# A decoder trunk on one core: the condition turned into columns on PE, the other vectors carried in the scale weights' rows

## The chip, the cores and the metric

The kernel runs on one core of one Trainium2 chip, in one launch. The metric is the device time of an execution in microseconds (us). A profile is one execution taken by the hardware profiler; in it PE is TensorE (PEld its weight loads), DVE is VectorE, ACT is ScalarE, POOL is GpSimd and SP is SyncE, which here only issues loads. Lines such as L354 are lines of the kernel before the change, unless the text says otherwise.

## The reference

One decoder layer on 512 tokens of width 1024, in float32. A condition vector `c` sets a shift, a scale and a gate for each of two sublayers. What the change touches is the first step of the first sublayer:

```python
cs = jax.nn.silu(c)
mod = cs @ w_ada[l] + b_ada[l]
shift1, scale1, gate1, shift2, scale2, gate2 = [m[:, None, :] for m in jnp.split(mod, 6, axis=-1)]
h = _rmsnorm(x, norm1_g[l]) * (1.0 + scale1) + shift1
proj = h @ w_in[l]
qa, ka, va, qd, kd, vd, ga, gd = jnp.split(proj, points, axis=-1)
```

`proj` then feeds two causal attention branches, one with a sliding window of 128 and learned sinks (8 heads, 2 key heads), one the difference of two softmax maps (4 heads). Each is projected to width 1024, they are merged by sigmoid gates `ga` and `gd`, projected once more and added to `x` times `gate1`. The second sublayer is an RMSNorm with `scale2` and `shift2`, and a gated MLP of width 2816 with a causal convolution of width 3 ahead of the GELU, added times `gate2`. A last RMSNorm ends it.

## The kernel before

Every large product is made of three: each float32 operand is split into a high part (rounded by a cast on ACT) and a low part (what is left, by a subtraction on DVE), and PE adds high·high, high·low and low·high.

The start of the kernel is written by hand, in the order in which each engine is to run it (`manual_schedule`). The features are cut into eight steps of 128 (k = 0 to 7). In this order:

- Loads. One load on ACT's queue brings `columns`, 128 rows of 161 numbers: `c` as 8 columns, the other vectors (biases, norm weights, convolution weights) as the rest, into the tile `cols`. SP's queue brings in turn the four pieces of the transposed `x` (`xT`), the shift weights of step 0 (`adaw0`, j = 1), its scale weights (`w_ada_0`, j = 0), the first 128 rows of the input projection (`w0`), and then the same three for each further step. Each of these is 512 KB.
- The condition. `cs` = silu of the 8 columns, made by an exponential on ACT and three steps on DVE (L255 to L258). PE repeats it along rows into two banks (L262), and DVE copies these to SBUF as `csb`. Ahead of that PE multiplies constants (`keep_warm`, L236).
- The norm of x. ACT squares the pieces of `xT` (L315), DVE adds the two halves of each (L316), and PE sums over features (`sums`, L304). A root on ACT and some small steps on DVE give one number per token, `rst`, which PE turns into a row (L340) in the bank `acc[7]`.
- Scale and shift of step 0. The scale comes from PE (`head_mod`, L296): eight products of `w_ada_0` with `cs`, five ahead of the turning of `rst` and three behind it, into `acc[3]`. The shift comes from DVE as two dot products with `csb` (`shift_half`, L325). Two DVE steps make of them the multiplier (L382) and the addend (L383) of `h`.
- `h` of step 0. DVE multiplies `xT` by the row of `rst` in two halves of 256 tokens (`scale_x`, L348), ACT applies multiplier and addend in two pieces (`h_tile`, L354; result `hThA`, the high part), then once more in full precision (`hf`), and copies the row of `rst` to SBUF (`rstb`, L388). DVE takes `hf` minus the high part (`h_low`).
- Products. 24 products a step into eight banks, `acc[0]` to `acc[7]` (in the trace aka, aqa, av, ava): eight with both high parts, eight with the weights' low part, eight with the low part of `h` (`mm_k`, L365 and L368). In step 0 the first three and the last of each eight take 128 tokens of `h` each (tokens 0 to 127, 128 to 255, 256 to 383 and 384 to 511); the other four take all 512.

For each further step ACT casts the weights (`split_hi`), makes multiplier and addend (`mod_end`, L279 and L280) from dot products on DVE (`mod_rows`), and `h`. What follows (attention, gates, the MLP) is ordered by a scheduler by priorities, with PE's stream again written out; the first two tiles of attention weights (`wqa`, cast at L120) are the first of it.

The lines at which the condition enters:

```python
nc.scalar.dma_start(cols[:, :NCOL], columns)
ccol, bsh, bsc1 = cols[:, 0:8], cols[:, 8:16], cols[:, 16:24]
keep_warm(10)
nc.scalar.activation(cs, ccol, AF.Exp, scale=-1.0)
```

Of the kernel before, what the change touches and what calls it, by code (L numbers as in the profile page):

```python
# [36 lines left out]
VA_AT = 5  # L37
SWA_FILL = (2, 1, 6, 2, 2, 2, 2, 5, 0)
DIFF_FILL = (3, 2, 4, 2)
NCOL = 161  # L40
# [7 lines left out]
def kernel(  # L48
# [4 lines left out]
    columns: bass.AP,  # L53
# [85 lines left out]

    cols = cpool.tile([P, NCOL + 32], F32, name="cols")  # L140
    nc.scalar.dma_start(cols[:, :NCOL], columns)
    ccol, bsh, bsc1 = cols[:, 0:8], cols[:, 8:16], cols[:, 16:24]
    blate, n1g, n2g = cols[:, 24:56], cols[:, 56:64], cols[:, 64:72]
    cv, sublnc = cols[:, 72:160], cols[:, 160:161]
# [108 lines left out]
    keep_warm(10)  # L253
# [40 lines left out]
    def head_mod(a0, a1):  # L294
        for a in range(a0, a1):
            nc.tensor.matmul(  # L296
                acc[3][:, :NB], adaw[0][:, 0, a * P : (a + 1) * P], cs[:, a : a + 1].to_broadcast([P, NB]),
                start=a == 0, stop=a == KT - 1,
            )
# [11 lines left out]
    for p in range(KT // 2):  # L311
        for hf in range(2) if p == 3 else (None,):
            sl = ALL if hf is None else HALVES[hf]
            sq, xx = (a.rearrange("p (a s) -> p a s", a=2)[:, :, sl] for a in (sqs[p], xT[:, p]))
            nc.scalar.activation(sq, xx, AF.Square)  # L315
# [13 lines left out]
    shift_half(0)  # L329
    r0 = pp.tile([P, NT], F32, tag="rs_c", bufs=3, name="r0")  # L330
# [7 lines left out]
    head_mod(0, 5)  # L338
    for t in range(NT):
        nc.tensor.transpose(acc[7][:, t * P : (t + 1) * P], rst[:, t : t + 1].to_broadcast([P, P]), ident)  # L340
    head_mod(5, KT)
# [37 lines left out]
    keep_warm(3)  # L379
    scale_x(0, HALVES[0])  # L380
    m = mods[0]
    nc.vector.tensor_scalar(m[:, 0:1], acc[3][:, 0:1], n1g[:, 0:1], cb[:, 0:1], ALU.mult, ALU.add)  # L382
    nc.vector.scalar_tensor_tensor(m[:, 1:2], m[:, 4:5], m[:, 5:6], bsh[:, 0:1], ALU.add, ALU.add)  # L383
    scale_x(0, HALVES[1])
    for sl in HALVES:
        h_tile(0, 0, sl)
# [1451 lines left out]
    "x", "x_t", "columns", "w_ada_0", "w_ada_t", "w_first", "w_tiles", "swa_sinks", "diff_lambda",  # L1838
# [40 lines left out]
```

## Time and profile before

| | |
|---|---|
| median of 3 runs | 677.56 us (676.93 to 678.12) |
| the profiled execution | 677.26 us, its span 675.4 us |
| PE busy | 665.2 us (98% of the span), 4021 instructions |
| DVE busy | 564.6 us (84%) |
| ACT busy | 400.2 us (59%) |
| POOL busy | 86.4 us (13%) |
| granted TensorE clock, mean | 0.996 |
| moved by DMA | 121.78 MB, mean 180 GB/s |

The span runs from the first to the last instruction; 1.86 us of the profiled execution lie outside it. A matmul's end is modelled, so a busy PE is not PE at its peak; but where PE is busy in every slice, the time is that of its instruction stream. In the chain of waits, read from the last instruction back, PE holds 88% of the span.

### The profile page before, as it was taken

Reading aid. Unit: us, or ns where it says so; the run is one execution under the profiler, and the core shown is the slowest. Engines: PE = TensorE matmul, PEld = TensorE weight load, DVE = VectorE, ACT = ScalarE, POOL = GpSimd, SP = SyncE. Lnnn points to the kernel's source line nnn. Section 1 sums busy time; section 2 is a strip of 40 time slices with the busy share of each in tenths; the row PEclk is TensorE's granted clock in tenths of the full one; section 3 lists DMA queues with packets and bytes.
Section 4 is the critical chain, followed back from the end, with each engine's and each line's share of the span. In section 5 each row is a group of like instructions: output and inputs, shape, how many; then the busy total and the mean of one; then the engine's idle time right before and its main releaser. Section 6 shows DMA issues by size and latency. Waiting matters only on the chain.

```text
span 675.4 us, 10796 instructions
## 1 busy us (share of the span) xinstructions
PE 665.2 (98%) x4021; PEld 591.2 (88%) x4021; DVE 564.6 (84%) x1006; ACT 400.2 (59%) x703; POOL 86.4 (13%) x111
## 2 busy tenths in 40 slices
PE   8999999999999999999999999999999999999995
PEld 7888888888888888888899999999999998888884
DVE  6997996778767688954899998888888899979996
ACT  6678787466645333233696655556655666665664
POOL 2000000002213200010010211011111004441200
PEclk9999999999999999999999999999999999999998
DMA  8962231355266798569275987897786559996803
GB/s 351 408 242 71 87 103 63 127 155 173 93 172 195 233 317 263 196 168 309 68 122 139 226 201 198 204 214 163 186 197 175 128 187 210 197 200 188 158 0 125
DMA packets 72068, 121.78 MB, mean 180 GB/s; under 512 B 4240, under 2 KB 48432, under 8 KB 72016
## 3 DMA queue, kind: packets, MB, share of 16 engines
q1 hardware_dynamic: 53104, 95.04, 41.6%
q0 software_dynamic: 18624, 25.84, 23.0%
q8 instruction: 31, 0.51, 0.3%
q10 hardware_dynamic: 288, 0.21, 0.1%
q14 instruction: 21, 0.17, 0.1%
HBM read 118.97 MB, written 2.11 MB: 179 GB/s over the span
## 4 chain that ended last, share of the span: by engine, by line
PE 88%; issue 7%; DVE 2%; POOL 1%; DMA 1%; ACT 0%; POOLq 0%
PE up L1202 33%; PE dc L1808 7%; PE av L368 3%; PE pga L123 2%; PE pga L125 2%; PE pga L124 2%; PE pgd L125 2%; PE oc L1258 2%; PE pgd L124 2%; PE oc L1259 2%; PE oc L1262 2%; PE pgd L123 2%; PE aqa L365 2%; PE sd L679 2%; PE sw L581 1%
## 5 line engine op out<-in xcount | busy, mean ns | idle before, releaser
L1202 PE MATMUL up<-t,m_whi 128*128 128x256 f32 x512 | 93.1, 283 | 0.0
L1202 PEld LDWEIGHTS up<-t,m_whi 128*128 128x128 f32 x512 | 79.9, 192 | 0.0
L1202 PE MATMUL up<-t,m_wlo 128*128 128x256 f32 x256 | 72.4, 283 | 0.0
L1202 PE MATMUL up<-bh,p_whi 128*128 128x256 f32 x232 | 65.7, 283 | 0.0
L1202 PE MATMUL up<-bl,p_whi 128*128 128x256 f32 x232 | 65.7, 283 | 0.0
L1202 PE MATMUL up<-bh,p_wlo 128*128 128x256 f32 x232 | 65.7, 283 | 0.0
L1202 PEld LDWEIGHTS up<-t,m_wlo 128*128 128x128 f32 x256 | 49.2, 192 | 0.0
L1104 POOL DMA_DIRECT2D s<-in_w_up_dram x21 | 27.0, 1368 | 157.6 <-DMA s<-in_w_up_dram 127.8
L1202 PEld LDWEIGHTS up<-bh,p_whi 128*128 128x128 f32 x232 | 44.5, 192 | 0.0
L1202 PEld LDWEIGHTS up<-bl,p_whi 128*128 128x128 f32 x232 | 44.5, 192 | 0.0
L1202 PEld LDWEIGHTS up<-bh,p_wlo 128*128 128x128 f32 x232 | 44.5, 192 | 0.0
L1132 ACT CAST m_whi<-s 128x1024 fp32r<-128x1024 f32 x31 | 32.5, 1047 | 15.7 <-DVE s L1126 9.1
L795 DVE CUSTOM_DVE_ANT_0 ra<-ra,csb 128x1024 f32<-128x1024 f32 x32 | 38.6, 1219 | 3.0 <-DMA ra<-in_w_ada_t_dram 3.0
L1136 DVE TENSOR_TENSOR m_wlo<-s,m_whi 128x1024 fp32r<-128x1024 f32 x31 | 37.8, 1218 | 1.3 <-ACT m_whi L1132 1.3
L1202 PE MATMUL up<-t,p_whi 128*128 128x256 f32 x176 | 32.2, 283 | 0.0
L1202 PEld LDWEIGHTS up<-t,p_whi 128*128 128x128 f32 x176 | 27.4, 192 | 0.1
L705 ACT ACTIVATE sd<-sd,dmx 128x128 f32<-128x128 f32 (+3 forms) x32 | 17.7, 555 | 14.9 <-DVE dmx L690 14.7
L1132 ACT CAST p_whi<-wa 128x1024 fp32r<-128x1024 f32 x18 | 18.8, 1043 | 12.6 <-DMA s<-in_w_up_dram 7.2
L1209 ACT ACTIVATE gT<-a,cols 128x512 f32<-128x512 f32 x22 | 17.6, 813 | 13.4 <-DVE a L1244 13.0
L1136 DVE TENSOR_TENSOR p_wlo<-wa,p_whi 128x1024 fp32r<-128x1024 f32 x18 | 22.0, 1222 | 4.0 <-ACT p_whi L1132 3.2
L1202 PE MATMUL up<-t,p_wlo 128*128 128x256 f32 x88 | 24.9, 283 | 0.0
L1126 DVE TENSOR_TENSOR s<-s,wa 128x1024 f32<-128x1024 f32 x20 | 24.4, 1218 | 0.1
(551 smaller groups left out, 2037.6 us busy)
## 6 DMA issues: line engine op xcount, KB each, us to landing
ra<-in_w_ada_t_dram SPq DMA_DIRECT2D x32, 512.0 KB, 4.7
wa<-in_w_up_dram SPq DMA_DIRECT2D x22, 512.0 KB, 4.3
s<-in_w_up_dram SPq DMA_DIRECT2D x21, 512.0 KB, 4.7
s<-in_w_up_dram POOLq DMA_DIRECT2D x21, 512.0 KB, 6.6
adaw<-in_w_ada_t_dram SPq DMA_DIRECT2D x15, 512.0 KB, 10.2
a<-in_w_up_dram SPq DMA_DIRECT2D x11, 512.0 KB, 4.9
b<-in_w_down_dram SPq DMA_DIRECT2D x10, 512.0 KB, 3.9
w<-in_w_first_dram SPq DMA_DIRECT2D x8, 512.0 KB, 10.2
```

Source lines behind the costliest of these rows:

```text
L123: nc.tensor.matmul(o, lh, rh, start=start, stop=False)
L124: nc.tensor.matmul(o, lh, rl, start=False, stop=False)
L125: nc.tensor.matmul(o, ll, rh, start=False, stop=stop)
L368: nc.tensor.matmul(acc[i], ht[:, t : t + P], wts[k][w][:, S:], start=start, stop=stop)
L705: nc.scalar.activation(pm[m], pm[m], AF.Exp, bias=mx[:, m : m + 1], scale=-1.0, accum_out=(l0, l1)[m])
L795: nc.vector.tensor_tensor_reduce(r, r, csb, 1.0, 0.0, ALU.mult, ALU.add, late_mod[:, idx : idx + 1])
L1104: nc.gpsimd.dma_start(dst, upblock(*blk), accum_op=ALU.add)
L1126: nc.vector.tensor_add(src, src, R[J, "a11" if name == "m6" else "a12"])
L1132: nc.scalar.copy(W[J, name][0], R[J, SRC[name]])
L1136: nc.vector.tensor_sub(lo, R[J, SRC[name]], hi.bitcast(F32))
L1202: nc.tensor.matmul(o[u], w[:, k, cu], b[:, k], start=name in ("p1", "m5", "p2") and k == 0 and x == 0, stop=k == 3 and x == 2, skip_group_ ...
L1808: nc.tensor.matmul((bank2[u] if o is None else o)[:, sl], a[:, q, cu], b[:, q, sl], start=first_mm and x == 0, stop=last_mm and x == 2, sk ...
```

## The change

`c` is no longer part of `columns`. It is loaded as it lies in memory, 8 rows of 128 numbers (`crow`, 4 KB, on ACT's queue), and PE transposes these rows into 8 columns of a bank that is free then (`acc[2]`), between six and three of the products of constants, which were ten in a row. ACT and DVE read the condition from the bank.

The other vectors, now 153 columns, stand behind the 1024 scale weights in the rows of `w_ada_0`; both come in one load into a tile of their own (`scale0`, 1177 numbers a row) by SP's queue, in the scale weights' place. GpSimd copies the 153 columns to `cols`, and does the scalings of some of them and the product `cb`, which DVE did before. `cols` keeps its size, and the tiles behind `scale0` begin at multiples of 64 bytes as before.

Around it the order changes: the squares of the first piece of `xT` are made in two halves; the second copy of `csb` goes ahead of the last square additions; the addend of `h` is computed ahead of the scaling of `xT`; `h` of step 0 is made in pieces of 128, 128 and 256 tokens.

```diff
-NCOL = 161
+NCOL = 153
...
-    cols = cpool.tile([P, NCOL + 32], F32, name="cols")
-    nc.scalar.dma_start(cols[:, :NCOL], columns)
-    ccol, bsh, bsc1 = cols[:, 0:8], cols[:, 8:16], cols[:, 16:24]
+    cols = cpool.tile([P, NCOL + 40], F32, name="cols")
+    bsh, bsc1 = cols[:, 0:8], cols[:, 8:16]
...
+    crow = big.tile([8, P], F32, tag="kvA", name="crow")
+    nc.scalar.dma_start(crow, c[0].rearrange("(k p) -> k p", p=P))
...
+    scale0 = pp.tile([P, D + NCOL], F32, name="scale0")
...
         for j in (1, 0):
-            src = w_ada_t[(1 - j) * D + k * P : (1 - j) * D + (k + 1) * P, :] if k or j else w_ada_0
-            nc.sync.dma_start(adaw[k][:, j], src)
+            if k or j:
+                nc.sync.dma_start(adaw[k][:, j], w_ada_t[(1 - j) * D + k * P : (1 - j) * D + (k + 1) * P, :])
+            else:
+                nc.sync.dma_start(scale0, w_ada_0)
...
-    keep_warm(10)
+    keep_warm(6)
+    ccol = acc[2][:, :8]
+    nc.tensor.transpose(ccol, crow, ident[:8, :8])
+    keep_warm(3)
...
-    nc.vector.tensor_scalar_add(bsc1, bsc1, 1.0)
-    nc.vector.tensor_scalar_mul(n1g, n1g, -0.5)
-    nc.vector.tensor_scalar_mul(sublnc, sublnc, -0.5 * (1.0 - LAM_INIT))
-    cb = cpool.tile([P, 8], F32, name="cb")
-    nc.vector.tensor_mul(cb, bsc1, n1g)
...
-                acc[3][:, :NB], adaw[0][:, 0, a * P : (a + 1) * P], cs[:, a : a + 1].to_broadcast([P, NB]),
+                acc[3][:, :NB], scale0[:, a * P : (a + 1) * P], cs[:, a : a + 1].to_broadcast([P, NB]),
...
-        for hf in range(2) if p == 3 else (None,):
+        for hf in range(2) if p in (0, 3) else (None,):
...
-        if p == 1:
-            nc.vector.tensor_copy(csb[:, :S], acc[0])
+        if p in (1, 2):
+            nc.vector.tensor_copy(csb[:, (p - 1) * S : p * S], acc[p - 1])
     root_table(sqs[3][:, 0:1])
-    nc.vector.tensor_copy(csb[:, S:], acc[1])
...
     shift_half(0)
+    head_mod(0, HEAD_A)
...
     shift_half(1)
-    head_mod(0, 5)
...
-    head_mod(5, KT)
+    head_mod(HEAD_A, KT)
+    nc.gpsimd.tensor_copy(cols[:, :NCOL], scale0[:, D:])
+    nc.gpsimd.tensor_scalar_add(bsc1, bsc1, 1.0)
+    nc.gpsimd.tensor_scalar_mul(n1g, n1g, -0.5)
+    nc.gpsimd.tensor_scalar_mul(sublnc, sublnc, -0.5 * (1.0 - LAM_INIT))
+    cb = cpool.tile([P, 8], F32, name="cb")
+    nc.gpsimd.tensor_mul(cb, bsc1, n1g)
...
+    m = mods[0]
+    nc.vector.scalar_tensor_tensor(m[:, 1:2], m[:, 4:5], m[:, 5:6], bsh[:, 0:1], ALU.add, ALU.add)
     scale_x(0, HALVES[0])
-    m = mods[0]
     nc.vector.tensor_scalar(m[:, 0:1], acc[3][:, 0:1], n1g[:, 0:1], cb[:, 0:1], ALU.mult, ALU.add)
-    nc.vector.scalar_tensor_tensor(m[:, 1:2], m[:, 4:5], m[:, 5:6], bsh[:, 0:1], ALU.add, ALU.add)
     scale_x(0, HALVES[1])
-    for sl in HALVES:
+    for sl in (slice(0, P), slice(P, 2 * P), HALVES[1]):
         h_tile(0, 0, sl)
```

`HEAD_A` is 5, so PE's order of head products and turned rows is the old one. Three places show what moves. First DVE between the second half of the shift (ISA, writing `adaw`) and the low part of the first weights (`wlo`), before and then after; `mod` is the tile of multiplier and addend:

```order
L325 ISA adaw_98,mod_203<-adaw_98,csb 128x512
L325 ISA mod_203 128x1
L348 TENSOR_TENSOR xT<-xT,av_147 128x256
L382 TENSOR_SCALAR mod_203<-av_143,cols,cb 128x1
L383 SCALAR_TENSOR_TENSOR mod_203<-mod_203,cols 128x1
L348 TENSOR_TENSOR xT<-xT,av_147 128x256
L289 TENSOR_TENSOR wlo_269<-w_0_101,whi_268 128x1024
```

and after the change:

```order
L327 ISA adaw_100,mod_200<-adaw_100,csb 128x512
L327 ISA mod_200 128x1
L389 SCALAR_TENSOR_TENSOR mod_200<-mod_200,cols 128x1
L356 TENSOR_TENSOR xT<-xT,av_149 128x256
L391 TENSOR_SCALAR mod_200<-av_145,cols,cb 128x1
L356 TENSOR_TENSOR xT<-xT,av_149 128x256
L292 TENSOR_TENSOR wlo_274<-w_0_103,whi_273 128x1024
```

The addend (L383, now L389) has moved ahead of the first scaling; only the multiplier still stands between the two scalings. Second ACT from the casts of the first weights (`whi`) to the next step's cast, before:

```order
L286 CAST whi_268<-w_0_101 128x512 x2
L354 ACTIVATE hThA<-xT,mod_203 128x256 x2
L354 ACTIVATE hf_280<-xT,mod_203 128x512
L388 COPY rstb<-av_147 128x512
L286 CAST whi_296<-w_1_106 128x1024
```

and after the change:

```order
L289 CAST whi_273<-w_0_103 128x512 x2
L362 ACTIVATE hThA<-xT,mod_200 128x128 x2
L362 ACTIVATE hThA<-xT,mod_200 128x256
L362 ACTIVATE hf_285<-xT,mod_200 128x512
L396 COPY rstb<-av_149 128x512
L289 CAST whi_302<-w_1_108 128x1024
```

One piece of 256 tokens has become two of 128. Third, at the end of the eight steps, ACT from the full `h` of step 6 to the second cast of attention weights, before:

```order
L354 ACTIVATE hf_489<-xT,mod_209 128x512
L286 CAST whi_519<-w_7_136 128x1024
L279 ACTIVATE mod_210<-mod_210,cb,cols 128x1
L280 ACTIVATE mod_210<-mod_210,cols 128x1
L354 ACTIVATE hThB<-xT,mod_210 128x512
L354 ACTIVATE hf_526<-xT,mod_210 128x512
L404 ACT_TABLE_LOAD
L404 ACTIVATE warm<-warm 128x1
L120 CAST wqa_h<-wqa_587 128x1024
L120 CAST wqa_h<-wqa_593 128x1024
```

and after the change:

```order
L362 ACTIVATE hf_495<-xT,mod_206 128x512
L289 CAST whi_525<-w_7_138 128x1024
L121 CAST wqa_h<-wqa_593 128x1024
L282 ACTIVATE mod_207<-mod_207,cb,cols 128x1
L283 ACTIVATE mod_207<-mod_207,cols 128x1
L362 ACTIVATE hThB<-xT,mod_207 128x512
L362 ACTIVATE hf_532<-xT,mod_207 128x512
L412 ACT_TABLE_LOAD
L412 ACTIVATE warm<-warm 128x1
L121 CAST wqa_h<-wqa_599 128x1024
```

The first of the two casts now stands ahead of step 7's multiplier and addend; on DVE the subtraction that belongs to it has moved in the same way, ahead of the low part of step 7's `h`. PE's stream behind the first product and the orders of all engines behind this place are the same as before.

More of the change, by code (lines that the diff above doesn't have):

```diff
@@ L37 @@
 VA_AT = 5
+HEAD_A = 5
 SWA_FILL = (2, 1, 6, 2, 2, 2, 2, 5, 0)
 DIFF_FILL = (3, 2, 4, 2)
-NCOL = 161
+NCOL = 153
 G1COL = NCOL + 16
@@ L52 @@
     x_t: bass.AP,
-    columns: bass.AP,
+    c: bass.AP,
     w_ada_0: bass.AP,
@@ L137 @@
     nc.gpsimd.memset(mhalf, -0.5)
-    cols = cpool.tile([P, NCOL + 32], F32, name="cols")
-    nc.scalar.dma_start(cols[:, :NCOL], columns)
-    ccol, bsh, bsc1 = cols[:, 0:8], cols[:, 8:16], cols[:, 16:24]
-    blate, n1g, n2g = cols[:, 24:56], cols[:, 56:64], cols[:, 64:72]
-    cv, sublnc = cols[:, 72:160], cols[:, 160:161]
+    cols = cpool.tile([P, NCOL + 40], F32, name="cols")
+    bsh, bsc1 = cols[:, 0:8], cols[:, 8:16]
+    blate, n1g, n2g = cols[:, 16:48], cols[:, 48:56], cols[:, 56:64]
+    cv, sublnc = cols[:, 64:152], cols[:, 152:153]
     sink = cpool.tile([P, 8], F32, name="sink")
@@ L1837 @@
 _INS = [
-    "x", "x_t", "columns", "w_ada_0", "w_ada_t", "w_first", "w_tiles", "swa_sinks", "diff_lambda",
+    "x", "x_t", "c", "w_ada_0", "w_ada_t", "w_first", "w_tiles", "swa_sinks", "diff_lambda",
     "w_branch_swa", "w_branch_diff", "w_out", "w_up", "w_down", "final_g",
@@ L1852 @@
         _np.asarray(inputs[name]).reshape(-1, P).T
-        for name in ("c", "b_ada", "norm1_g", "norm2_g", "conv_w", "conv_b", "diff_subln_g")
+        for name in ("b_ada", "norm1_g", "norm2_g", "conv_w", "conv_b", "diff_subln_g")
     ]
     laid = dict(inputs)
-    laid["columns"] = _np.concatenate(by_column, axis=1)
     laid["w_ada_t"] = _np.asarray(inputs["w_ada"])[0].T
@@ L1859 @@
     ada = _np.asarray(inputs["w_ada"])[0].reshape(KT, P, -1, P)
-    laid["w_ada_0"] = ada[:, :, KT].transpose(1, 0, 2).reshape(P, D)
+    laid["w_ada_0"] = _np.concatenate([ada[:, :, KT].transpose(1, 0, 2).reshape(P, D)] + by_column, axis=1)
     w = _np.asarray(inputs["w_in"])[0]
```

## The prediction

> **What bounds the kernel now.** I read the busy time by stretch first, to see where an engine has anything to give, and after it the chain of waits at the start, where the change lies. Columns are the stretch, its length, busy us (and instructions) of PE, its weight loads, DVE, ACT and POOL, then PEclk, DMA share, GB/s.
>
> ```profile
> 0.00:16.00 16.00, 13.59 (x91) 12.27 (x92) 9.59 (x30) 10.51 (x17) 3.88 (x22) 1.00 0.89 348
> 16.00:21.00 5.00, 5.00 (x23) 3.79 (x22) 5.00 (x8) 3.23 (x8) 0.00 (x0) 1.00 1.02 406
> 21.00:54.00 33.00, 33.00 (x146) 27.32 (x146) 30.07 (x46) 22.24 (x35) 0.00 (x0) 1.00 0.75 286
> ...
> 500.00:640.00 140.00, 140.00 (x865) 126.54 (x864) 128.48 (x183) 87.97 (x129) 31.59 (x27) 1.00 0.82 183
> ```
>
> From 16 us on PE is busy without a hole and stays so: the end of the kernel is the moment at which the stream of products starts, plus a fixed length of PE work. So the change is worth what it moves in that start, one for one and no more. The chain shows what the start hangs on (start us, us, what):
>
> ```profile
> 0.73 4.11 DMA cols<-in_columns_dram
> ...
> 4.86 0.21 ACT cs L255
> ...
> 9.13 2.05 PE av L304 x16
> 11.18 1.35 PE av L296 x10
> 12.54 0.59 PE av L340 x4
> 13.13 0.68 PE av L296 x6
> ...
> 14.28 0.61 ACT hThA L354
> ...
> 14.93 0.99 PE av L368 x3
> ```
>
> It begins with the load of the columns. But a chain names one releaser a step, and three engines stop inside it for something else:
>
> ```profile
> 8.56 1.15 ACT L315 ACTIVATE sq<-xT 128x512 f32<-128x512 f32 x2 [0.21 <-DMA xT<-in_x_t_dram]
> ...
> 11.15 1.19 PEld L296 LDWEIGHTS av<-cs,adaw 128*128 128x128 f32 x10 [0.16 <-DMA adaw<-in_w_ada_dram]
> ...
> 12.41 1.14 ACT L286 CAST whi<-w 128x512 fp32r<-128x512 f32 x2 [0.86 <-DMA w<-in_w_first_dram]
> ```
>
> The squares wait for the last piece of x (landed about 8.5), the scale products for the scale's weights (about 11.1), the first cast for the first weights (about 12.35). All three come down one saturated SP queue, in that order. Behind the second lie 1.35 + 0.59 + 0.68 us of PE, which end at 13.81, and that number starts everything later.
>
> **The change, part by part.** *The condition.* The 80 KB of columns leave the ACT queue and 4 KB take their place. Queue q10 in the window 2.5 to 3 us, then in 4 to 4.5, then both queues over the first 10 us (packets, MB, share of 16 engines):
>
> ```profile
> q10 hardware_dynamic: 19, 0.01, 20.8%
> ...
> q10 hardware_dynamic: 31, 0.01, 9.2%
> ...
> q1 hardware_dynamic: 819, 3.03, 77.9%
> q10 hardware_dynamic: 144, 0.08, 3.4%
> ```
>
> The queue's first packets run between 2.5 and 3 us, its last between 4 and 4.5, and the landing is at 4.84. Eight rows should therefore land between 3.0 and 4.84; I take 3.3, nearer the first packets. With about 0.35 for the transpose and its hand-over (estimated from the 0.59 us of four such transposes and the gaps of the chain) the condition is ready 1.2 us earlier, and at the worst 0.35 later. Neither reaches the products: the 16 sums that end at 11.18 wait for the squares of x, and the scale products behind them for their weights. What goes is cover, not path. The second copy of the condition's rows now stands ahead of the last two square adds on DVE and gives back some of what an earlier x gains there.
>
> *The queue.* q10 took 3.4% of 10 us, so 0.34 us of all engines, out of the way of x. The 153 columns come back as 612 bytes on each of 128 rows of the scale load: 0.078 MB at 3.03 MB per 7.79 us is 0.20 us, if a row stays one packet, and about the old 0.34 if it is cut. The scale's weights land 0 to 0.14 us earlier: I take 0.1 gained for everything from 11.15 on.
>
> *The start of h.* DVE and ACT around it:
>
> ```profile
> 12.34 0.68 DVE L325 CUSTOM_DVE_ANT_0 adaw<-adaw,csb 128x512 f32<-128x512 f32 x1
> ...
> 13.16 0.42 DVE L348 TENSOR_TENSOR xT<-xT,av 128x256 f32<-128x256 f32 x1
> 13.84 0.28 DVE L382 TENSOR_SCALAR mod<-av,cols,cb 128x1 f32<-128x1 f32 x1 [0.25 <-PE av L296]
> 14.03 0.21 DVE L383 SCALAR_TENSOR_TENSOR mod<-mod,cols 128x1 f32<-128x1 f32 x1
> 14.16 0.41 DVE L348 TENSOR_TENSOR xT<-xT,av 128x256 f32<-128x256 f32 x1
> ...
> 14.28 1.09 ACT L354 ACTIVATE hThA<-xT,mod 128x256 fp32r<-128x256 f32 x2 [0.72 <-DVE mod L383]
> 15.28 0.80 ACT L354 ACTIVATE hf<-xT,mod 128x512 f32<-128x512 f32 x1
> 15.98 0.56 ACT L388 COPY rstb<-av 128x512 f32<-128x512 f32 x1
> ```
>
> With the addend (L383) ahead of the scaling, in DVE's idle time before 13.84, ACT follows the multiplier's end, 13.84 + 0.28 = 14.12, so it starts at 14.15 and not 14.28: 0.13 gained, and the second scaling starts 0.13 earlier too. Then ACT makes three pieces of h instead of two. Two pieces of 256 columns took 1.00 from start to start (14.28 to 15.28), 0.50 each; 512 columns 0.70 (15.28 to 15.98). That is 0.30 fixed and 0.10 for each 128 columns, so a piece of 128 takes 0.40, and three take 0.40 + 0.40 + 0.50 = 1.30. The first product gains 0.13 + 0.10 and starts near 14.6, 0.33 earlier with the queue's 0.1. But the third product needs columns of the last piece: that ends 0.30 − 0.13 = 0.17 later than now, 0.07 with the queue. PE runs gapless from there, so its stream starts 0.07 *later*: the early first product only lengthens a gap behind it. Bounds of the piece: as cheap as 0.25 (half of 256 columns) the stream starts 0.23 earlier, at 0.50 it is 0.27 later.
>
> *GpSimd.* Copying the columns out of the scale load, three scalings and `cb` move from DVE at 5.6 us, where nobody waited, to GpSimd behind the scale load at 11.1, and the multiplier waits for the last of them. Rows of such operations (min/median/max ns, and when):
>
> ```profile
> L749 POOL TENSOR_TENSOR dls<-dls x4: 525/988/1049, 132.4 to 207.1; 128x4 f32<-128x4 f32 x4
> ...
> L750 POOL TENSOR_SCALAR dls<-dls x4: 225/228/251, 133.6 to 208.2; 128x4 f32<-128x4 f32 x4
> ...
> L757 POOL TENSOR_SCALAR rt<-rt x4: 231/352/1075, 153.8 to 220.9; 128x4 f32<-128x4 f32 x4
> ...
> L245 POOL TENSOR_SCALAR_AFFINE_SELECT dsw<-dsw 128x256 f32<-128x256 f32 x1 | 0.4, 398 | 0.1
> ```
>
> At their best: at most 0.40 for the copy, 3 × 0.23, 0.53 and five gaps of some 0.06 make 1.9 us, ready at 13.0, under the 13.84 at which DVE wants it. That is 0.8 us of cover, and DVE runs one long two-input pass in it (12.34, 0.68 us). The likely cost is nothing, or a few tenths if both meet or if GpSimd holds up DVE's short steps to `rst`; I put 0.05.
> The Trainium skill (SBUF — State Buffer, "SBUF: two separate sides") says that GpSimd shares a pair of ports with DVE operations that read two SBUF inputs, and that whoever is first holds it for a whole instruction. L757's spread, 231 to 1075 ns for one shape, agrees; by that rule one pass of 0.68 at worst is added to 13.0, which still leaves 0.1.
>
> *The first attention weights.* Their cast moves to the place before the last layer step's multiplier:
>
> ```profile
> L470 SPq DMA_DIRECT2D wqa<-in_w_tiles_dram x2: 328/328/328, 34.5 to 39.2; - x2
> ...
> DMA to landing us min/median/max: 4.3/6.0/7.7
> ...
> 47.32 0.39 ACT L279 ACTIVATE mod<-mod,cb,cols 128x1 f32<-128x1 f32 x1 [1.56 <-DVE mod L275]
> ...
> 50.87 1.99 ACT L120 CAST wqa_h<-wqa 128x1024 fp32r<-128x1024 f32 x2
> ...
> 49.48 0.69 DVE L357 TENSOR_TENSOR hTlB<-hf,hThB 128x512 fp32r<-128x512 f32 x1 [1.06 <-ACT hf L354]
> ...
> 51.67 0.23 PE aka L365
> ```
>
> Issued at 34.5 and landed by 42.2, it is there; 1.0 us of cast fits into ACT's 1.56 of idle time at 47.3, and its DVE half into the 1.06 before 49.48, with some 0.1 over. PE reads that low part at 51.67, 1.4 us after it is done. No cost; without that cover it would be 0.1.
>
> The sum: −0.10 + 0.17 + 0.05 = +0.1 us. The profiled execution took 677.26 (span 675.4 and 1.86 around it), so 677.36 by its own time. It lies 0.30 under the median of the three runs, 677.56; the same step from there is 677.66. I predict 677.4, no difference: a measurement of this kernel can tell about 0.2%, 1.35 us.
>
> **The rivals.** *The condition was the limit.* If the chain is right as printed, its first link loses 1.2 us and all of it reaches the products: 676.1. For it speaks the 4.11 us at the head of the chain; against it the three waits for DMA behind it, and that PE's scale products follow a load that moves by 0.14 at most. 676.1 is just past 0.2% under the median. Chance 0.08.
>
> *GpSimd late (the other side).* If its five operations run at the long ends of the rows, 0.40 + 3 × 1.08 + 1.05 + 0.3 = 5.0 us, the multiplier waits till 16.1 and not 13.84: +2.3 us, 679.6. It decides from the point where the five take over 2.7 us (13.84 − 11.1). Against it: the long ends come from stretches where DVE runs long passes back to back, while here it has one of 0.68. Over 1.35 us late: chance 0.07; between 0.2 and that: 0.08.
>
> *PE slows down in the new gaps.*
>
> ```profile
> 2.00:3.00 1.00, 1.00 (x7) 1.00 (x7) 0.00 (x0) 0.65 (x2) 0.74 (x6) 1.00 0.60 156
> ...
> 10.00:11.00 1.00, 1.00 (x11) 0.99 (x9) 1.00 (x3) 1.00 (x1) 0.00 (x0) 1.00 1.02 410
> ```
>
> PE gets through 7 instructions in the third us and 11 in the eleventh. If the condition lands near 4.84, PE idles between the two groups of constants and might stay slow: 2.62 us of work behind the scale load would take 11/7 of that, +1.5 us: 678.8, at the edge of 0.2%. Today's hole before the condition's rows, 4.9 to 5.9, cost no speed. Chance 0.03.
> The Trainium skill (TensorE: Matmul & The Clock Gate, "The HAM clock gate") asks for about 3.4 us of idleness before the clock falls back; by that rule no gap here is long enough.
>
> **How the numbers follow.** The forecast, the stream's start moved by −0.4 to +0.4, has 0.74. The range takes the bounds of the pieces and of GpSimd's middle case round both bases, and the spread of the runs (676.93 to 678.12): 676.4 to 678.5. Faster by over 0.2% (under 676.2) needs nearly all of the condition's rival: 0.07 of its 0.08. Slower (over 678.9) takes GpSimd's 0.07 and PE's 0.03: 0.10. Within: 0.83.
>
> **What would show it.** Right: the condition's rows on PE about 1 us earlier, head products still behind the scale load near 11.0, first product near 14.6 with a longer gap before the third, and the same PE work behind. Wrong: the scale load landing well before 10.9 or after 11.3; DVE idle before the multiplier with GpSimd as releaser; pieces of 128 columns under 0.3 us apart; or any new PE gap after 21 us.

## The result: 0.25% slower, and the profile after

The changed kernel takes 679.18 us (median of 16 runs, 677.98 to 680.12); the kernel before takes 677.31 us beside it on the same chip (16 runs). The ratio is 1.0025 with a 95% interval of 1.0018 to 1.0032. The prediction was 677.4 us, 676.4 to 678.5, most likely no difference. So it was wrong: the change costs 1.9 us. The profiled execution took 678.79 us, of which the span is 676.6 and 2.19 lie outside it (2.18 to 2.28 in all 16 runs). The profile before had 1.86 outside.

The stretches first, in the columns of the table shown of before:

```profile
0.00:16.00 16.00, 13.99 (x88) 12.61 (x88) 9.22 (x27) 10.26 (x18) 5.06 (x27) 1.00 0.90 349
16.00:21.00 5.00, 5.00 (x22) 4.06 (x23) 5.00 (x8) 3.45 (x7) 0.00 (x0) 1.00 1.03 418
21.00:54.00 33.00, 33.00 (x145) 26.96 (x144) 30.48 (x46) 22.49 (x36) 0.00 (x0) 1.00 0.79 300
...
500.00:640.00 140.00, 140.00 (x867) 126.66 (x866) 128.41 (x184) 88.57 (x130) 31.59 (x28) 1.00 0.83 183
```

PE is as full as before, the granted clock is 1.00, and no new gap shows. At this width everything looks like before. The difference lies in four places, each too small for the table. The first is the start. These are rows of the timeline: start us, busy us, and in brackets the idle time before and what ended it.

```profile
7.51 1.06 ACT L318 ACTIVATE sq<-xT 128x1024 f32<-128x1024 f32 x1 [1.06 <-DMA xT<-in_x_t_dram]
...
8.75 1.15 ACT L318 ACTIVATE sq<-xT 128x512 f32<-128x512 f32 x2 [0.18 <-DMA xT<-in_x_t_dram]
...
11.48 1.19 PEld L299 LDWEIGHTS av<-cs,scale 128*128 128x128 f32 x10 [0.24 <-DMA scale<-in_w_ada_dram]
...
12.55 0.20 POOL L349 TENSOR_TENSOR cb<-cols 128x8 f32<-128x8 f32 x1
...
14.16 0.28 DVE L391 TENSOR_SCALAR mod<-av,cols,cb 128x1 f32<-128x1 f32 x1 [0.19 <-PE av L299]
...
14.48 1.37 ACT L362 ACTIVATE hThA<-xT,mod 128x128 fp32r<-128x128 f32 x3 [0.58 <-DVE mod L391]
...
15.02 1.37 PE L376 MATMUL av<-whi,hThA 128*128 128x512 f32 x3 [0.30 <-ACT hThA L362]
...
15.75 0.80 ACT L362 ACTIVATE hf<-xT,mod 128x512 f32<-128x512 f32 x1
```

The last piece of x lands 0.2 us later than before (8.75 against 8.56) and the scale's weights 0.33 later (11.48 against 11.15), although the columns no longer go on the other queue. GpSimd ends its five operations at 12.75, long before DVE wants `cb` at 14.16; the multiplier waits for PE. The three pieces of `h` take 14.48 to 15.75.

Of the two late loads it is x that sets the pace. `rst`, which is made from the squares of x, is turned into a row as soon as DVE has it, before the change:

```profile
12.26 0.16 DVE L168 SCALAR_TENSOR_TENSOR rst<-rt,r 128x4 f32<-128x4 f32 x1
...
12.48 0.65 PE L340 MATMUL av<-ident,rst 128*128 128x128 f32 x4
```

and after it:

```profile
12.51 0.17 DVE L168 SCALAR_TENSOR_TENSOR rst<-rt,r 128x4 f32<-128x4 f32 x1
...
12.73 0.65 PE L342 MATMUL av<-ident,rst 128*128 128x128 f32 x4
```

Both times PE begins 0.06 us behind the end of `rst`, and has begun the last of the scale products ahead of it by then (at 12.26 and 12.59; they come 0.11 us apart). So the turning is 0.25 us late. The fourth product of step 0, the first that needs all of `h`, starts at 16.23 and not 15.76: 0.47 late.

The second place is the eight steps. PE's rows of one and the same pair of products in steps 3, 4 and 5 (timeline), of the kernel before:

```profile
32.93 0.62 PE L368 MATMUL av<-whi,hThA 128*128 128x512 f32 x2
...
38.37 0.62 PE L368 MATMUL av<-whi,hThA 128*128 128x512 f32 x2
...
43.81 0.62 PE L368 MATMUL av<-whi,hThA 128*128 128x512 f32 x2
```

and of the changed one:

```profile
33.45 0.63 PE L376 MATMUL av<-whi,hThA 128*128 128x512 f32 x2
...
39.00 0.61 PE L376 MATMUL av<-whi,hThA 128*128 128x512 f32 x2
...
44.49 0.63 PE L376 MATMUL av<-whi,hThA 128*128 128x512 f32 x2
```

Before, a step is 5.44 us long each time. After, from step 3 to 4 it is 5.55, from 4 to 5 5.49. By single products the spacing is 232 ns in odd steps; in even ones it is 227, as before, but for the first eight products (229). From the first product of step 1 to the last of step 7 that makes 0.59 us (38.44 against the 37.85 of the padded kernel below). PE never idles here, so a busy column cannot show it.

In step 1 the opposite happens. The weight loads of its first products, before and then after the change:

```profile
20.49 0.30 PEld L368 LDWEIGHTS av<-whi,hThA 128*128 128x128 f32 x2 [0.18 <-ACT hThA L354]
20.99 0.19 PEld L368 LDWEIGHTS av<-whi,hThA 128*128 128x128 f32 x1 [0.20 <-ACT hThA L354]
```

```profile
20.81 0.65 PEld L376 LDWEIGHTS av<-whi,hThA 128*128 128x128 f32 x3
```

The kernel before waits twice for `h` of step 1, and that step takes 5.55 us and not 5.44. The changed kernel does not wait. The table of stretches counts PE as busy there, since the ends of its products are modelled. In sum the products from the fourth of step 0 to the last of step 7 take 43.25 us and not 42.78.

The third place is the end. Of the kernel before, first the last piece of the chain (start, us: GpSimd's issue of an output):

```profile
671.04 0.61 POOLq L1875
```

then the DMA view from 660 us to the end (of queues packets, MB and share of 16 engines, of issues KB each and the us to landing):

```profile
q14 instruction: 2, 0.02, 0.2%
...
out_dram<-x POOLq DMA_DIRECT2D x1, 128.0 KB, 2.8
out_dram<-x ACTq DMA_DIRECT2D x1, 128.0 KB, 2.8
```

The same piece of the chain of the changed kernel:

```profile
671.64 0.61 POOLq L1882
```

and its DMA view from 660 us on:

```profile
q14 instruction: 3, 0.02, 0.5%
...
out_dram<-x POOLq DMA_DIRECT2D x1, 128.0 KB, 3.3
out_dram<-x ACTq DMA_DIRECT2D x1, 128.0 KB, 3.6
```

At the last product of step 7 the changed kernel is 0.94 us behind (59.48 against 58.54), at the last output's issue 0.60. What takes up the 0.34 in between was not followed; two profiles of the kernel before differ by 0.3 there (651.85 and 651.55 us from the fourth product to PE's end). From the issue to the span's end it takes 4.93 and not 4.32 us: the output's transfers land later. Queue q14, whose packets the profile calls "instruction", runs one 8 KB packet more, and one of them now runs while the output leaves. The fourth place is outside the span: 0.33 more. Start and steps 0.60, end 0.61 and outside 0.33 are the 1.5 us between the two profiled executions.

### The profile page after: what moved, and what is told of

Same layout as the page of the kernel before. It is cut to its first block, busy times and chain, and to the rows that moved or that the text cites. A ratio compares the mean times of both kernels' runs of the same rounds, so it can differ in the third digit from the quotient of the medians.

```text
span 676.6 us, 10797 instructions
## 1 busy us (share of the span) xinstructions
PE 666.2 (98%) x4020; PEld 592.1 (88%) x4020; DVE 564.7 (83%) x1003; ACT 400.7 (59%) x705; POOL 86.0 (13%) x116
## 4 chain that ended last, share of the span: by engine, by line
PE 88%; issue 7%; DVE 2%; DMA 1%; POOL 1%; SPq 0%; POOLq 0%; ACT 0%; DVEq 0%
PE up L1210 33%; PE dc L1816 7%; PE av L376 3%; PE pga L124 2%; PE pga L126 2%; PE pga L125 2%; PE oc L1267 2%; PE pgd L124 2%; PE oc L1266 2%; PE pgd L125 2%; PE oc L1270 2%; PE pgd L126 2%; PE aqa L373 2%; PE sd L687 2%; DMA scale<-in_w_ada_dram 1%
## 5 line engine op out<-in xcount | busy, mean ns | idle before, releaser
L1144 DVE TENSOR_TENSOR p_wlo<-wa,p_whi 128x1024 fp32r<-128x1024 f32 x18 | 22.0, 1224 | 4.0 <-ACT p_whi L1140 3.8
```

The costliest lines, as they stand in the source:

```text
L1144: nc.vector.tensor_sub(lo, R[J, SRC[name]], hi.bitcast(F32))
```

## The experiments

All times are medians beside runs of the kernel before on the same chip, which took 677.09 to 677.31 us from group to group of runs. An interval of a ratio is about 0.0009 (0.6 us) to either side, so steps of 0.4 us rest on the traces beside the medians.

**The kernel before, unchanged,** as a measure of what two builds of one program differ by.

> The kernel before, unchanged, to learn what one execution and its trace vary by. Expected: ratio 1.000 within its interval; product to product 226.7 ns in all steps from 2 on; first product near 14.9 us; scale weights landed near 11.1 us; span about 675.4 and 1.86 us outside it. If the later landing of the scale weights in the changed kernel (11.44) and its longer wait for the last output (GpSimd's last drain 4.1 us instead of 3.5) are chance, this run shows such values too; if they belong to the change, it shows 11.1 and 3.5 again.

677.09 us, ratio 1.0003 [0.9994, 1.0012]. First scale product at 11.14, GpSimd's last wait 3.50 us, 1.89 us outside the span: the later values of the changed kernel do not show here.

**The addresses of the odd steps' weights.** `scale0` is the first tile of the pool `p1`, and the weights of the odd steps lie in that pool, those of the even steps elsewhere. In the compiled program of the kernel before, the odd weights begin at byte 200064 of a partition (384 modulo 512, as the even steps' weights and the `h` operand do). In the changed one they begin 4736 bytes further, at 204800, a multiple of 512. First an unused tile of 4736 bytes put ahead in the kernel before:

```diff
+    pad0 = pp.tile([P, 1184], F32, name="pad0")
+    nc.gpsimd.memset(pad0[:, 0:1], 0.0)
```

> The kernel before with an unused tile of 4736 bytes ahead of the others in the first pool, so that the odd steps' weight tiles begin where they do in the changed kernel (at 0 instead of 384 modulo 512 bytes). Address theory: the products of odd steps take about 232 ns instead of 226.7, the even ones stay at 226.7; 96 products by 5.3 ns make +0.5 us by the end of the steps, ratio about 1.0005 to 1.0008. Rival (the slow products come from the change's other traffic, the loads or GpSimd): all steps stay at 226.7, ratio 1.000.

677.77 us, ratio 1.0010 [1.0001, 1.0018]. The same pair of products as above:

```profile
32.97 0.63 PE L370 MATMUL av<-whi,hThA 128*128 128x512 f32 x2
...
38.52 0.61 PE L370 MATMUL av<-whi,hThA 128*128 128x512 f32 x2
...
44.01 0.63 PE L370 MATMUL av<-whi,hThA 128*128 128x512 f32 x2
```

5.55 and 5.49 us, as in the changed kernel: the address alone does it. (The tile's one write adds an instruction to GpSimd's program, and 0.15 of the longer time lies outside the span; see below on the end.) Then the reverse, the changed kernel with the scale's tile widened to 5120 bytes:

```diff
-    scale0 = pp.tile([P, D + NCOL], F32, name="scale0")
+    scale0_wide = pp.tile([P, 1280], F32, name="scale0")
+    scale0 = scale0_wide[:, : D + NCOL]
```

> The changed kernel with its scale tile widened from 4708 to 5120 bytes, so that the tiles behind it begin at 384 modulo 512 bytes as in the kernel before; what is loaded stays the same. Address theory: odd steps back to 226.7 ns, PE's stream 0.5 us shorter than in the changed kernel, ratio about 1.0018 instead of 1.0025; the rest of the loss (later start of the stream, the end, what lies outside the span) stays. Rival (other traffic): odd steps stay at 232 ns and the ratio at 1.0025.

678.68 us, ratio 1.0019 [1.0010, 1.0028]: 0.5 less than the change, and all eight steps at 227 ns. From the first product of step 1 to the last of step 7 it is 37.85 us, against 38.44 in the changed kernel. Two widths more tell which property of the address counts, 1216 and 1248 columns:

> The changed kernel with the scale tile at 1216 columns, 4864 bytes: the weights of the odd steps begin at 128 modulo 512 bytes. If tiles at multiples of 256 are slow to stream, or only tiles at multiples of 512, the products of the odd steps come every 227 ns; if the weights must lie as the h operand does (384 modulo 512), every 232 ns.

> The changed kernel with the scale tile at 1248 columns, 4992 bytes: the weights of the odd steps begin at 256 modulo 512 bytes. If tiles at multiples of 256 are slow: 232 ns. If only multiples of 512 are slow: 227 ns. If the weights must lie as the h operand does: 232 ns.

One profile each. PE's rows of the pair in steps 3 to 5 with 1216 columns:

```profile
33.30 0.61 PE L377 MATMUL av<-whi,hThA 128*128 128x512 f32 x2
...
38.74 0.61 PE L377 MATMUL av<-whi,hThA 128*128 128x512 f32 x2
...
44.18 0.61 PE L377 MATMUL av<-whi,hThA 128*128 128x512 f32 x2
```

and with 1248:

```profile
32.60 0.62 PE L377 MATMUL av<-whi,hThA 128*128 128x512 f32 x2
...
38.15 0.62 PE L377 MATMUL av<-whi,hThA 128*128 128x512 f32 x2
...
43.63 0.62 PE L377 MATMUL av<-whi,hThA 128*128 128x512 f32 x2
```

At 128 modulo 512 a step is 5.44 us, at 256 modulo 512 it is 5.55 and 5.48. With the two others (384 fast, 0 slow) that describes the four: weights that begin at a multiple of 256 bytes were slow beside an `h` that begins at 128 modulo 256. Whether that is the address itself or its place against the other operand was not tried, nor were tiles at 64 modulo 128.

**The pieces of h.** The padded kernel with the `h` of step 0 in two halves again:

```diff
-    for sl in (slice(0, P), slice(P, 2 * P), HALVES[1]):
+    for sl in HALVES:
```

> As the one with the wider scale tile, and step 0's h made in two pieces of 256 tokens again. Theory of the pieces: three pieces cost 0.17 us against two at the third product; with two, the third product follows the first by the old 0.57 us or less and PE's stream starts about 0.2 us earlier than with three. Rival (the late third product comes from the later scale weights alone): the distance from scale weights' landing to the fourth product is the same with two pieces as with three.

678.80 us, ratio 1.0018 [1.0009, 1.0027]: no gain in the time. In the traces, from the multiplier's start (DVE) to the fourth product of step 0 it takes 2.08 us with three pieces and 1.80 with two, so the three cost 0.28 at the start. But with two pieces the stop in step 1 is back: that step takes 5.55 us and not 5.44, so 0.17 of the 0.28 is left. A time with an interval of 0.6 us to either side cannot show that. Besides, the scale load lands at 12.21 us in this profile and at 10.95 in the padded one; this variation is taken up below.

**The end.** The compiled programs hold, for the kernel before and the changed one, 1225 and 1220 instructions on VectorE and 192 and 197 on GpSimd (waits, branches and DMA issues among them; the traces record 1223 and 1218, 191 and 196). First four small constants more on VectorE at the start of the padded kernel, which makes 1224:

```diff
+    for _ in range(4):
+        nc.vector.memset(hold, 0.0)
```

> The changed kernel with the scale tile at 1280 columns, and four small constants more on VectorE at the very start, so that VectorE runs as many instructions as in the kernel before. Theory (the last output waits because VectorE's next block of instructions, now four instructions later in its program, is fetched while the output leaves): the second fetch goes back from 5.0 to about 3.4 us behind PE's last product, GpSimd's last wait from 4.3 to 3.5 us, the time from 678.7 to about 678.1, and the 2.25 us outside the span stay. Rival (GpSimd's longer program or the new input layout makes the end long): the wait stays at 4.0 to 4.3 us and the time at 678.7.

678.30 us, ratio 1.0013 [1.0005, 1.0022]. GpSimd's wait for its last output, 3.54 us before, 4.11 in the changed and 4.31 in the padded kernel, is 3.72. The second packet of q14 at the end is back at 3.1 us behind the start of PE's last product (3.1 before, 5.0 in the two others), ahead of the output. Outside the span it is still 2.20. Then five of the eight small constants of the attention scales from GpSimd to VectorE, 1225 and 192 instructions:

```diff
-        nc.gpsimd.memset(qsc[0:64, i : i + 1], 2.0 ** (i - 2))
-        nc.gpsimd.memset(qsc[64:128, i : i + 1], 2.0 ** (i + 2))
+        (nc.gpsimd if i < 1 else nc.vector).memset(qsc[0:64, i : i + 1], 2.0 ** (i - 2))
+        (nc.gpsimd if i < 2 else nc.vector).memset(qsc[64:128, i : i + 1], 2.0 ** (i + 2))
```

> The changed kernel with the scale tile at 1280 columns, and five of the eight small constants for the attention scales written by VectorE and no longer by GpSimd: GpSimd runs as many instructions as in the kernel before, VectorE one more. Theory: as in the run with four more VectorE instructions the last wait is 3.5 us; and the third fetch behind the span is gone and the time outside the span 1.9 us and not 2.25, so 677.7 us. Rival (the time outside the span hangs on the inputs or on the whole program's size): outside stays at 2.2, 678.1 us.

677.91 us, ratio 1.0010 [1.0001, 1.0019], 1.89 outside the span. The DMA view from 660 us on with the four more on VectorE:

```profile
q14 instruction: 3, 0.02, 0.3%
...
out_dram<-x POOLq DMA_DIRECT2D x1, 128.0 KB, 3.0
```

and with the five moved:

```profile
q14 instruction: 2, 0.02, 0.2%
...
out_dram<-x POOLq DMA_DIRECT2D x1, 128.0 KB, 2.9
```

Making VectorE's program as long as before ends the late landing, making GpSimd's as short as before takes the third packet and the 0.33 us outside away. It goes with the count in every kernel that was timed here: 192 instructions on GpSimd give a median of 1.87 to 1.92 us outside, 193 give 2.01 and 2.04 (two kernels: the unused tile above and the long rows below), 197 give 2.20 to 2.24. In all 17 profiles the two go together: where the second packet runs 3.1 to 3.2 us behind the start of PE's last product (11 profiles, VectorE at 1224 or 1225 instructions) the span ends 7.7 to 7.9 us behind that product's end, and where it runs at 5.0 to 5.4 (6 profiles, VectorE at 1220) 8.2 to 8.7. That the packets are blocks of these two engines' programs is inferred from what moved them.

**The addend alone,** ahead of the scaling, in the kernel before:

```diff
+    m = mods[0]
+    nc.vector.scalar_tensor_tensor(m[:, 1:2], m[:, 4:5], m[:, 5:6], bsh[:, 0:1], ALU.add, ALU.add)
     scale_x(0, HALVES[0])
-    m = mods[0]
     nc.vector.tensor_scalar(m[:, 0:1], acc[3][:, 0:1], n1g[:, 0:1], cb[:, 0:1], ALU.mult, ALU.add)
-    nc.vector.scalar_tensor_tensor(m[:, 1:2], m[:, 4:5], m[:, 5:6], bsh[:, 0:1], ALU.add, ALU.add)
```

> The kernel before with one part of the change alone: the addend's instruction ahead of the first scaling, two pieces of h. By the traces so far (scale products' start to fourth product 4.61 us in the kernel before, 4.44 in the changed one with two pieces) the stream of products starts 0.17 us earlier: 676.9 against 677.1 for the kernel before. If the rest of the start sets it, 4.61 and 677.1.

677.07 us, ratio 0.9999 [0.9990, 1.0008]. The stretch from scale product to fourth product is 4.48 us, not 4.61. But this stretch also shrinks when only the scale's load lands later (4.46 in the kernel with long rows below, which leaves the addend where it was), so it is no measure of the addend. The one from the multiplier's start to the fourth product is: 1.80 us here and 1.92 in the four profiles with the addend behind it. The addend's move brings 0.12, too small for the time to show.

**The scale's load.** Two experiments on the long rows. The vectors in a load of their own again, on the other queue behind the condition's, in the padded kernel:

```diff
+    nc.scalar.dma_start(cols[:, :NCOL], columns)
...
-                nc.sync.dma_start(scale0, w_ada_0)
+                nc.sync.dma_start(scale0[:, :D], w_ada_0)
...
-    nc.gpsimd.tensor_copy(cols[:, :NCOL], scale0[:, D:])
```

> The changed kernel with the scale tile at 1280 columns, but the vectors in a load of their own again, behind the condition's on the same queue: rows of the scale's weights of 4096 bytes. Theory (rows of 4708 bytes make the scale's load land late or at times that vary, 10.9 to 12.2): first scale product at 11.0 to 11.2, spans within 1.2 us of each other as in the kernel before, against 1.9 now. Rival (the condition's load, or chance, does it): landing and spread as before this step, and the time stays at 678.7.

678.37 us, ratio 1.0022 [1.0013, 1.0030]. The first scale product starts at 11.00, and the spans of its runs lie within 1.3 us (675.9 to 677.2; 675.4 to 677.3 with the padding alone). The time itself is not shown to fall: 0.3 us less than the padded kernel in the median, and a ratio that is no lower. And the long rows alone in the kernel before:

```diff
+    scale0 = pp.tile([P, 1280], F32, name="scale0")
...
-            nc.sync.dma_start(adaw[k][:, j], src)
+            nc.sync.dma_start(adaw[k][:, j] if k or j else scale0[:, : D + 153], src)
```

> The kernel before with one thing changed: each row of the scale's weights carries 153 columns more, 4708 bytes in place of 4096, which nobody reads, in a tile of its own at 1280 columns; the load of the columns and all instructions stay. Theory (long rows make the scale's load land later): the first scale product starts at 11.3 to 12.2 us and not at 11.05 to 11.4, and the time rises by 0.2 to 0.8 us to 677.4 to 678.0. Rival (the extra 0.078 MB cost only their 0.20 us of a full queue; the late landings of the changed kernel are chance or come from the condition's load): 11.2 to 11.5, 677.3.

677.19 us, ratio 0.9999 [0.9990, 1.0008], first scale product at 11.35: the rival. Long rows delay the scale by their bytes, 0.2 us, and hardly anything of that reaches the products: the fourth starts at 15.81 and not 15.76, since x, which sets the pace, lands nearly as before (8.62 against 8.56). My theory of the late load fell here, and it was the load taken away from the other queue that was left to suspect. **All four causes undone at once,** condition as rows and addend kept:

> The changed kernel with all that has been found undone at once, the condition as rows and the addend ahead of the scaling kept: scale tile at 1280 columns, five small constants from GpSimd to VectorE, the vectors in a load of their own, the h of step 0 in two halves. Theory (these four explain the whole difference): 677.1 or up to 0.2 below it, as the kernel before, 1.9 us outside the span, last wait 3.5 us. Rival (something else of the change costs too): 677.4 to 677.9.

676.97 us, ratio 0.9999 [0.9990, 1.0008], first scale product at 10.83, 1.87 outside. Nothing else of the change costs anything that can be measured, and what is kept of it brings nothing that can be: no version here beats the kernel before. Then three kernels that differ from this one only around the vectors' load. Their load on SP's queue behind the scale's (short rows, only 4 KB on the other queue):

```diff
-    nc.scalar.dma_start(cols[:, :NCOL], columns)
...
                 nc.sync.dma_start(scale0[:, :D], w_ada_0)
+                nc.sync.dma_start(cols[:, :NCOL], columns)
```

> The kernel with all four found causes undone, but the vectors' load put on the same queue as x and the weights, right behind the scale's load: rows of 4096 bytes, and only the condition's 4 KB on the other queue. If it is the missing second load beside x that makes packets of x stall: first scale product at 11.3 to 12.2 us, the spans spread over 1.5 us or more, 677.5. If it is the long rows, or the place of the arrays in memory: 10.7 to 11.0, 676.9 to 677.1.

678.01 us, ratio 1.0011 [1.0002, 1.0020], first scale product at 11.77, spans from 675.0 to 677.2. Next the vectors in the long rows as in the change, with an array of them among the inputs that is not loaded:

> The changed kernel with the scale tile at 1280 columns, five small constants moved to VectorE and two halves of h, the vectors in the scale's rows as in the change; and beside it an array of the vectors among the inputs, as in the kernel before, that is not loaded. If the place of the arrays in memory makes packets stall: no stall, first scale product at 10.9 to 11.2, 677.1. If not: 11.3 to 12.2, 677.6, no different from the changed kernel.

677.90 us, ratio 1.0006 [0.9997, 1.0015], first scale product at 12.28. And that array loaded, for nobody, on the other queue:

```diff
+    spare = big.tile([P, NCOL], F32, tag="kvB", name="spare")
+    nc.scalar.dma_start(spare, columns)
```

> As the run before it, but the array of the vectors is also loaded, behind the condition's load on the other queue, into a tile that nobody reads: rows of 4708 bytes and a second load beside x. If the missing second load is the cause: no stall, 11.0 to 11.3, 677.1 to 677.3. If the long rows are: 11.3 to 12.2, 677.6.

677.08 us, ratio 0.9997 [0.9989, 1.0006], first scale product at 11.00, spans within 0.8 us: a load that nobody needs makes the kernel 0.8 us faster (677.62 to 678.48 us without it, 676.86 to 677.68 with it, 11 runs each on the same chip). The table of stretches shows where. Last columns: granted clock, DMA share, GB/s. The kernel before:

```profile
4.00:5.00 1.00, 1.00 (x9) 0.97 (x7) 0.00 (x0) 0.14 (x2) 0.93 (x3) 1.00 1.05 418
5.00:6.00 1.00, 0.30 (x4) 0.17 (x3) 0.83 (x7) 1.00 (x2) 0.06 (x2) 1.00 1.03 418
```

the changed one:

```profile
4.00:5.00 1.00, 1.00 (x6) 0.98 (x6) 0.50 (x1) 0.71 (x3) 0.93 (x3) 1.00 0.94 356
5.00:6.00 1.00, 1.00 (x6) 1.00 (x6) 0.93 (x5) 1.00 (x2) 0.04 (x1) 1.00 0.95 352
```

the vectors on SP's queue:

```profile
4.00:5.00 1.00, 1.00 (x6) 0.98 (x6) 0.43 (x3) 0.71 (x3) 0.30 (x2) 1.00 0.81 295
5.00:6.00 1.00, 1.00 (x6) 1.00 (x6) 0.87 (x3) 1.00 (x2) 0.00 (x0) 1.00 0.89 299
```

long rows without a second load (the array that is not loaded):

```profile
4.00:5.00 1.00, 1.00 (x8) 0.98 (x7) 0.42 (x3) 0.70 (x3) 0.28 (x2) 1.00 0.94 320
5.00:6.00 1.00, 1.00 (x11) 0.88 (x10) 0.88 (x3) 1.00 (x2) 0.00 (x0) 1.00 0.65 262
```

and the same with a load that nobody reads:

```profile
4.00:5.00 1.00, 1.00 (x6) 0.98 (x6) 0.43 (x3) 0.71 (x3) 0.28 (x2) 1.00 1.00 372
5.00:6.00 1.00, 1.00 (x6) 1.00 (x6) 0.87 (x3) 1.00 (x2) 0.00 (x0) 1.00 1.03 419
```

With 80 KB on the other queue the transfer of x keeps its rate or soon has it again; in the three profiles shown without it the rate is 15 to 37% under that of the kernel before between 4 and 6 us. Of the nine profiles without such a load, eight have single packets of x that take 0.7 to 1.5 us there, where 0.16 is usual, and land the scale at 11.34 to 12.28; the ninth, the padded kernel, has none and landed at 10.95. Of the eight profiles with it, none has a packet of x over 0.52 us, and the scale lands at 10.83 to 11.39. So the load away does not make every execution late, but most. Row length and the place of the arrays in memory are out as causes. Why the second load keeps the first one going stays open.

The Trainium skill (DMA: Bandwidth & Descriptors, "Issuing engines are not separate DMA queues") says that transfers issued from several engines share the same DMA engines, and that starting them from several engines saves only the sequencer's time to start them. By that rule the place of an 80 KB load among the queues should not matter beside its bytes. It mattered here: for the same bytes on SP's queue the median is 0.70 us above that of the kernel before on the same chip, on the other queue 0.12 below it (678.01 and 676.97 us).

The ladder of medians, each line with the edits above it kept. The runs come from several chips, so the third column takes off the median of the kernel before on the same chip, and the steps are those of that column:

| kernel | us | above the kernel before | step |
|---|---|---|---|
| the change | 679.18 | 1.87 | |
| scale tile at 5120 bytes | 678.68 | 1.46 | −0.41 |
| four more instructions on VectorE | 678.30 | 1.10 | −0.36 |
| five instructions of GpSimd to VectorE instead | 677.91 | 0.71 | −0.39 |
| two pieces of `h`, array among the inputs | 677.90 | 0.59 | −0.12 |
| 80 KB beside x on the other queue | 677.08 | −0.23 | −0.82 |

All steps but the last are smaller than the interval of a single time; the traces beside them and the run with all undone carry the account.

## Why the prediction was wrong

*What bounds the kernel.* The reading that the condition is not the limit was right: its rows on PE came 0.23 us earlier (5.63 against 5.86) and not 1 us. PE turns it only behind six constants at 3.98, so its silu begins 0.57 us earlier (4.29 against 4.86), and 0.34 of that goes between there and the rows. The step that failed is the sentence that the end is the products' start plus a fixed length of PE work, so that the change is worth what it moves in that start "and no more". The start itself moved by 0.47 us, where the sum had 0.1, and that is only a part of the 1.9. The PE work was not fixed: the addresses made it 0.59 us longer without a hole in PE, and 0.11 came back in step 1, where the kernel before had a stop that the reading "busy without a hole" missed. And the end behind PE was not fixed: 0.61 us more from the last output's issue to the span's end, and 0.33 more outside the span. I read the change only where its lines stand. A tile put first in a pool moves every tile behind it, and instructions added or dropped at the start move all that follow in their engine's program.

*The queue, −0.10.* This term had the wrong sign. The sum of bytes was right (long rows alone: the scale 0.2 us later, as worked out). That it moves "everything from 11.15 on" was not: of those 0.2 only 0.05 reached the fourth product, since PE turned `rst` when DVE had made it and not when the scale products let go. What was missing is that the 80 KB beside x were worth more than their own 0.34 us of the engines: without them the load of x stalls in most executions, and the change loses about 0.8 in the medians of two pairs of kernels (in a third, the padded one, 0.3 or nothing). Taking away a load that looked free was the largest single cost; why it helps stays open.

*The pieces, +0.17.* Right in mechanism and nearly in size: three pieces took 1.27 us (14.48 to 15.75) where 1.30 was worked out. From the multiplier's start to the fourth product it is 1.92 us before and 2.07 after: +0.15, of which the pieces are +0.27 and the addend −0.12. What the sum left out is that 0.11 of it comes back in step 1. The first product comes 1.09 us behind the multiplier's start before and 0.86 after, which is the 0.23 that was worked out; it starts later all the same (15.02 against 14.93), since the multiplier does.

*GpSimd, +0.05.* The five operations took 1.25 us with their gaps, not 1.9, and nobody waited for them: 0. Its cost came from the five instructions as such, at the other end of the kernel. The rival's price (679.6) and sign are near what happened, its mechanism is not.

*The cast of the attention weights, 0.* All steps undone at once gave the time of the kernel before with this move still in, so it costs nothing that can be measured.

*The rivals.* Neither the condition's (676.1) nor the one of a PE that slows in the gaps came. Behind the gaps PE is as fast as before: ten weight loads of the scale products take 1.19 us in both kernels. (The column of the granted clock reads 1.00 from the start in both, also while PE gets through only 6 or 7 instructions a microsecond, so it could not have told.)

*The range.* It took in the bounds of each term and the spread of the runs, but no term for what was not listed. The steps of the ladder sum to 2.1 us; the largest term of the prediction's sum was 0.17.

## What to carry to other kernels

When a change adds a tile or shifts instructions, look at what stands behind it in the same pool and in the same engine's program: after it, compare the spacing of the products step by step and the transfers at the end, since neither shows as idle time. A load that is removed as superfluous may have been keeping its neighbour's rate up; compare the GB/s of the stretch in which it ran before you count its bytes as gained. And measure a piece of the start from the operation that releases it: a stretch that begins at another one changes with the slack between the two.

## What the hardware showed that was not expected

- Products whose weights begin at a multiple of 256 bytes of a partition came every 232 ns and not every 227, with the other operand at 128 modulo 256 (four offsets seen). That the tiles began at multiples of 64 bytes did not protect from it.
- The time outside the span grows with GpSimd's program: 1.89 us with 192 instructions, 2.01 to 2.04 with 193, 2.20 to 2.24 with 197, and a further 8 KB packet of queue q14 runs then. An 8 KB packet of that queue during the last output went with a span that ended 8.2 to 8.7 us behind PE and not 7.7 to 7.9.
- With 80 KB on a second queue beside a saturated load, and nothing else changed, the rate of all loads was 372 GB/s and not 320 from 4 to 5 us, and 419 and not 262 from 5 to 6. One profile without such a load shows no stall, so this holds for most executions and not for all.
